# A gated hybrid block on one core: merge steps spread over half jobs, the last gate group as one job of four tiles, loads of y, x and A21 at other places

## The chip, the cores and the metric

The kernel runs on one core of a Trainium2 chip. The metric is device time in microseconds of one execution; the runs shown are three executions of the kernel before, and one more execution of it was profiled. Five engines work side by side on the core, each through its own instructions in order: TensorE (PE in the profile), VectorE (DVE), ScalarE (ACT), GpSimd (POOL) and SyncE (SP), which here only issues DMA transfers. One engine waits for another where an instruction needs what the other has not yet written, or a place that it has not yet freed.

## The reference

One layer over 512 tokens of width 2048, in float32. The normalised input is multiplied by a wide matrix `w_in`; its columns feed two mixers and their gates. Mixer A is a gated linear recurrence with 8 heads of 128. Mixer B is attention with 8 heads over keys that a small indexer picks, with a position bias. Both outputs are projected to 2048 columns, merged by sigmoid gates, projected once more, added to the input and normalised:

```
y_a = hgrn2_branch(a_q, a_f, a_i, a_g, lb_all[layer], gnorm_a[layer])
y_b = dsa_branch(c_q, c_kv, k_idx_raw, w_idx_raw, b_g, ..., w_ukv[layer], ..., rel_bias, topk)
merged = (jax.nn.sigmoid(m_a) * (y_a @ w_pa[layer])
          + jax.nn.sigmoid(m_b) * (y_b @ w_pb[layer]))
x = x + merged @ w_out[layer]
...
return rmsnorm(x, final_norm_w)
```

## The kernel before, in words

**Products.** Each float32 operand is split into a high part (a cast, ACT, L67) and a low part (a subtraction, DVE, L68), and each product is three matmuls: high by high, low by high, high by low (`mm3`, L71 to L73). Tiles of results hold 128 rows by 512 columns and lie in eight banks: four named acc and four others, from which the recurrence and the attention draw too.

**Weights.** All weights come in blocks of 512 KB, listed in `specs` in the order of use. `load` (L125) asks for a block on SP's queue; there are two places `wr` for raw blocks. `prep(i)`, called before block i is used, makes sure that the blocks up to i+2 are split (places `wh`, `wl`, three each) and that loads up to two blocks further are asked for. SP works through its queue in order: a transfer that must wait for its place holds up every transfer behind it.

**Jobs and lanes.** The program is a list of jobs, run one after the other. A job made by `feat_job` multiplies one group of weight columns (`ntile` tiles of 128) with the transposed input: for every block, for every tile, for every 128 rows k of the block, the three matmuls, and after every tile of a block one `pump()`. A pump advances each of six lanes by one step; a lane holds generators, and every `yield` is the end of a step. So the small work of the recurrence (`hgrn_gen`) and of the attention (`att_gen`) is put between the matmuls of the large jobs, one step per pump, and the matmuls between two pumps are the only work that PE has while the other engines carry out a step. In a job of two tiles with blocks of four k, there are 2 pumps per block and 12 matmuls between two pumps. Stores are asked for two pumps after the step that makes the data.

**The stages that the change touches.** The last input columns, four gate tiles (44 to 47), are made by two jobs of two tiles, each with four blocks of four k; during them the recurrence of the last pair of heads ends and the attention of pair 2 runs. Then `uqkv(3)` makes queries, keys and values of the last head pair (its second weight block is the only one from `w_ukv`). In the second gate job, after its second block, `end_x` (all steps of the recurrence are forced out) frees the places of the first half of the transposed input, and asks for all of `ya` (8 transfers of 512 KB) on SP's queue. Eight jobs of two tiles multiply with `w_pa`, and during the first of them the attention of the last pair runs. Eight jobs multiply with `w_pb`.

**Attention steps.** `att_gen` handles two heads of a pair, c = 0 and 1: `att_scores` (matmuls, maximum on DVE, two yields, Exp on ACT at L827, scale on DVE at L830), then two yields, then `att_turn` (transposes on PE, into banks tA, tB, tC, L841), two yields, `att_values`.

**Merge.** Each `w_pb` job has two tiles and two blocks, so four pumps, and 48 matmuls. Its evacuation `pb_evac` multiplies each tile with its gate (DVE, L1169, into `mg`), adds the tile of branch A on GpSimd (L1170), and puts `merge_pair` in the lane misc: three casts of the merged pair into operand tiles (ACT, L1143 to L1146), their low parts (DVE, L1145 to L1149), one step later four sums for the seven product scheme of the output (DVE, L1154 to L1157, `sv`), their cast and low part (`so`). `mg` has six places; each job uses four, loaded at L1106 by `load_gates`, which is listed after each job.

**Output.** `out_job` multiplies the merged matrix with `w_out`. The first 1536 columns are three column blocks, each of eight units of 42 matmuls of 256 columns: a scheme of seven products whose result tiles fill seven banks. `block_evac` combines them into `os`. The last 512 columns use eight more weight blocks; the last four are kept, so that the four token tiles end one after the other, and each is normalised and stored while the next is multiplied. For that, the remaining input columns `x` are loaded (`xr`) and added by `rest(t)`: one DVE addition of 1536 columns (L1255) and one ACT sum of squares (L1257). The low half operand A21 was written to memory by `merge_pair`, and is loaded back (L1234).

## Time and profile before

| quantity | value |
|---|---|
| three runs | 1454.05, 1455.7, 1457.64 us; median 1455.7 us |
| the profiled execution's own time | 1456.32 us |
| its span | 1454.5 us |
| mean granted clock of TensorE | 0.989 |
| PE busy | 1404.2 us (97% of the span) |
| DVE, ACT, POOL busy | 1055.6, 607.1, 114.1 us |
| HBM read, written | 163.63 MB, 31.99 MB |

By stage, from the view that sums each engine's busy time in stretches of the span:

| stretch of the span, us | what runs | PE busy | DVE busy | ACT busy | POOL busy |
|---|---|---|---|---|---|
| 986 to 1067 | two gate jobs, last uqkv | 75.32 | 45.89 | 35.75 | 14.01 |
| 1067 to 1168 | eight w_pa jobs | 98.67 | 47.30 | 29.59 | 7.20 |
| 1168 to 1261 | eight w_pb jobs | 90.97 | 56.35 | 30.30 | 17.77 |
| 1261 to 1277 | first units of out_job | 7.54 | 12.66 | 5.80 | 2.51 |
| 1277 to 1392 | the other units | 113.21 | 95.81 | 44.22 | 0.00 |
| 1392 to 1447 | last 512 columns, final norm | 48.49 | 30.02 | 21.02 | 0.00 |
| 1447 to 1454.5 | last stores | 0.00 | 1.93 | 2.54 | 0.00 |

In the rows of the timeline, the first number is when an instruction starts, in microseconds from the span's start, the second how long it takes (of a row with x2, the whole group), and the brackets hold how long the engine had been idle and what ended that. A busy PE may still run at a lower clock; the granted clock, 1.00 at full speed, stands in the view of stretches.

### The profile page before, as it was taken

To read this page: it belongs to the slowest core of one execution; us is meant where nothing else is said; L and a number is where in the kernel's file an instruction comes from. 1 tells how busy PE (TensorE), PEld (TensorE's weight loads), DVE (VectorE), ACT (ScalarE), POOL (GpSimd) and SP (SyncE) were. 2 spreads that over 40 slices of the span, in tenths; PEclk is the share of its full clock that TensorE was granted. 3 is DMA by queue.
4 is the path that set the end of the run, shared out by engine and by line. 5 is a ranking of instruction groups with operands and counts; after the bars stand their busy time and mean duration, and the time that the engine had idled before them with its cause. 6 is when DMAs were issued, how large, how long until landed. Compare 5 with 4: busy or idle time off the path is not lost.

```text
span 1454.5 us, 25789 instructions
## 1 busy us (share of the span) xinstructions
PE 1404.2 (97%) x10604; PEld 1278.5 (88%) x10604; DVE 1055.6 (73%) x1716; ACT 607.1 (42%) x856; POOL 114.1 (8%) x103
## 2 busy tenths in 40 slices
PE   7999999999999999999999999999989999799996
PEld 7888999999999999988989889888768887599985
DVE  6697888889888886776979757658445346789845
ACT  5545444444444443662252542544443123343334
POOL 3100000000000000000202203204010012100000
PEclk9999999999999999999999999999999999999998
DMA  6233344444444444335242342342575655533373
GB/s 209 74 90 112 113 120 145 131 130 145 132 132 131 132 121 126 101 99 154 65 125 81 109 130 85 112 127 78 188 276 173 202 176 187 173 105 113 115 276 130
DMA packets 140647, 197.30 MB, mean 136 GB/s; under 512 B 9793, under 2 KB 86130, under 8 KB 140402
## 3 DMA queue, kind: packets, MB, share of 16 engines
q1 hardware_dynamic: 139138, 193.48, 42.9%
q8 instruction: 83, 1.36, 0.4%
q10 hardware_dynamic: 1392, 2.18, 0.4%
q14 instruction: 34, 0.28, 0.1%
HBM read 163.63 MB, written 31.99 MB: 134 GB/s over the span
## 4 chain that ended last, share of the span: by engine, by line
PE 68%; DVE 16%; ACT 6%; DMA 5%; issue 3%; POOL 1%; SPq 1%; ACTq 0%; DVEq 0%; POOLq 0%
PE pp L71 10%; PE pp L73 10%; PE pp L72 10%; PE acc L71 9%; PE acc L72 9%; PE acc L73 9%; DVE wl L68 4%; ACT wh L67 2%; PE hl L76 1%; PE acc L76 1%; DMA mg<-gate_d 1%; POOL mg L1170 1%; DVE sv L138 1%; PE ho L76 1%; DMA wr<-in_w_ukv_dram 1%
## 5 line engine op out<-in xcount | busy, mean ns | idle before, releaser
L68 DVE TENSOR_TENSOR wl<-wr,wh 128x1024 fp32r<-128x1024 f32 x118 | 145.9, 1237 | 100.9 <-ACT wh L67 100.7
L67 ACT ACTIVATE wh<-wr 128x1024 fp32r<-128x1024 f32 x118 | 124.3, 1054 | 190.7 <-PE acc L73 54.3
L67 ACT ACTIVATE wh<-sv 128x1024 fp32r<-128x1024 f32 x112 | 118.4, 1057 | 165.1 <-DVE sv L140 152.6
L71 PE MATMUL acc<-xh,wh 128*128 128x512 f32 x432 | 173.2, 401 | 0.0
L73 PE MATMUL acc<-xh,wl 128*128 128x512 f32 x432 | 168.6, 390 | 0.0
L72 PE MATMUL acc<-xl,wh 128*128 128x512 f32 x432 | 168.2, 389 | 0.0
L68 DVE TENSOR_TENSOR wl<-sv,wh 128x1024 fp32r<-128x1024 f32 x112 | 137.3, 1226 | 27.4 <-ACT wh L67 27.2
L71 PE MATMUL pp<-sh,wh 128*128 128x256 f32 x528 | 149.7, 284 | 2.4 <-ACT c L483 1.7
L73 PE MATMUL pp<-sh,wl 128*128 128x256 f32 x528 | 149.5, 283 | 0.0
L72 PE MATMUL pp<-sl,wh 128*128 128x256 f32 x528 | 149.4, 283 | 0.0
L67 ACT ACTIVATE bh<-wr 128x768 fp32r<-128x768 f32 x112 | 94.0, 839 | 129.0 <-issue 59.2
L68 DVE TENSOR_TENSOR bl<-wr,bh 128x768 fp32r<-128x768 f32 x112 | 106.9, 954 | 31.3 <-ACT bh L67 30.5
L71 PEld LDWEIGHTS pp<-sh,wh 128*128 128x128 f32 x528 | 101.3, 192 | 3.1 <-ACT c L483 1.9
L73 PEld LDWEIGHTS pp<-sh,wl 128*128 128x128 f32 x528 | 101.3, 192 | 0.1
L72 PEld LDWEIGHTS pp<-sl,wh 128*128 128x128 f32 x528 | 101.3, 192 | 0.0
L73 PE MATMUL pp<-xh,bl 128*128 128x256 f32 x352 | 99.7, 283 | 0.5 <-DVE bl L68 0.5
L72 PE MATMUL pp<-xl,bh 128*128 128x256 f32 x352 | 99.6, 283 | 0.0
L71 PE MATMUL pp<-xh,bh 128*128 128x256 f32 x352 | 99.6, 283 | 0.0
L71 PEld LDWEIGHTS acc<-xh,wh 128*128 128x128 f32 x432 | 81.1, 188 | 18.0 <-issue 1.8
L73 PEld LDWEIGHTS acc<-xh,wl 128*128 128x128 f32 x432 | 81.1, 188 | 17.5
L72 PEld LDWEIGHTS acc<-xl,wh 128*128 128x128 f32 x432 | 81.2, 188 | 17.3 <-issue 1.4
L138 DVE TENSOR_TENSOR sv<-wr 128x512 f32<-128x512 f32 x112 | 76.9, 686 | 0.8
(385 smaller groups left out, 3729.0 us busy)
## 6 DMA issues: line engine op xcount, KB each, us to landing
wr<-in_w_in_dram SPq DMA_DIRECT2D x154, 512.0 KB, 3.7
wr<-in_w_out_dram SPq DMA_DIRECT2D x32, 512.0 KB, 3.8
mg<-gate_d SPq DMA_DIRECT2D x48, 256.0 KB, 3.4
gate_d<-c SPq DMA_DIRECT2D x44, 256.0 KB, 4.0
wr<-in_w_pa_dram SPq DMA_DIRECT2D x16, 512.0 KB, 5.6
wr<-in_w_pb_dram SPq DMA_DIRECT2D x16, 512.0 KB, 5.2
x<-in_x_dram SPq DMA_DIRECT2D x8, 512.0 KB, 6.8
wr<-in_w_qidx_dram SPq DMA_DIRECT2D x8, 512.0 KB, 4.2
```

Source lines behind the costliest of these rows:

```text
L67: A.activation(hi, src, AF.Copy)
L68: V.tensor_tensor(lo, src, hi.bitcast(F32), op=OP.subtract)
L71: PE.matmul(ps, lh, rh, start=first, stop=False, skip_group_check=True)
L72: PE.matmul(ps, lh, rl, start=False, stop=False, skip_group_check=True)
L73: PE.matmul(ps, ll, rh, start=False, stop=last, skip_group_check=True)
L76: PE.matmul(ps, l, r, start=first, stop=last, skip_group_check=True)
L138: V.tensor_tensor(sv[:, 0:2, :], b[:, 1:3, :], b[:, 0:1, :].to_broadcast([128, 2, 256]), op=OP.add)
L1170: G.tensor_tensor(u, u, g, op=OP.add)
```

## The change

1. `att_gen` has one more `yield` ahead of each `att_turn`.
2. The four gate tiles 44 to 47 are one job of four tiles with eight blocks of two k. There are four pumps per block, 32 in all, with 6 matmuls between two of them (before, 16 pumps with 12). The places of the transposed input come free after blocks 1, 3, 5 and 7, and `ya` is asked for in three parts: heads 0 to 3 after block 1, 4 and 5 after block 3, 6 and 7 after block 5, where the recurrence is forced out (`end_hgrn`).
3. `merge_pair` begins with a yield. The four sums come first (into a tile of `R.v0` instead of `sv`), then the casts; the cast of the sums and the low parts follow one step later, the sums' low part in the last step. The addition of branch A in `pb_evac` moves from GpSimd to DVE.
4. In `out_job`, the last 512 columns of `x` are asked for at its start. A21 is asked for after the third unit of the third column block, `x` for tile 0 and the norm's weights (now on SP's queue) after its fifth, `x` of tiles 1 and 2 after that column block, of tile 3 after `rest(0)`. `rest(0)` and `rest(1)` stand at the third and fourth weight block, `rest(2)` and `rest(3)` at the token tiles 0 and 1.

```diff
@@ att_gen
         MB = att_bias(2 * p + 1)
         yield
         yield
+        yield
         PT = att_turn(P)
...
         P = yield from att_scores(p, 1, MB)
+        yield
         yield
         yield
         PT = att_turn(P)
@@ gate_job
-    def gate_job(j0, after=None):
+    def gate_job(j0, after):
...
-        feat_job(w_in, GATE_COL[j0], 2, NK, 4, x_rhs, evac, after=after)
+        feat_job(w_in, GATE_COL[j0], 4, NK, 2, x_rhs, evac, after=after)
...
-    gate_job(44)
-    gate_job(46, {1: lambda: end_x(), 3: lambda: take_x("yb", 2)})
...
+    def end_hgrn():
         drain("hgrn")
         flush()
         flush()
         leave("hgrn")
         R.u = enter("us", side="right")
-        take_x("ya", 0)
-        load_y(R.ya, ya_d, 0, H)
+        load_y(R.ya, ya_d, 6, 8)
+
+    gate_job(44, {1: lambda: (take_x(R.ya, 0), load_y(R.ya, ya_d, 0, 4)),
+                  3: lambda: (take_x(R.ya, 1), load_y(R.ya, ya_d, 4, 6)),
+                  5: lambda: (end_hgrn(), take_x(R.yb, 2)),
+                  7: lambda: take_x(R.yb, 3)})
@@ merge_pair
+        d = R.v0.tile([128, 4, 256], F32, name="hv")
+        yield
+        V.tensor_tensor(d[:, 0, :], a21, a22, op=OP.subtract)
+        V.tensor_tensor(d[:, 2, :], a11, a21, op=OP.subtract)
+        V.tensor_tensor(d[:, 1, :], d[:, 0, :], a11, op=OP.subtract)
+        V.tensor_tensor(d[:, 3, :], d[:, 1, :], a12, op=OP.add)
         A.activation(mh[:, 0, :], a11, AF.Copy)
         A.activation(mh[:, 1:3, :], two, AF.Copy)
+        A.activation(last[0], a21, AF.Copy)
+        yield
+        A.activation(sums[:, 0], d, AF.Copy)
         V.tensor_tensor(ml[:, 0, :], a11, mh[:, 0, :].bitcast(F32), op=OP.subtract)
-        A.activation(last[0], a21, AF.Copy)
-        yield
         V.tensor_tensor(ml[:, 1:3, :], two, mh[:, 1:3, :].bitcast(F32), op=OP.subtract)
...
         yield
-        d = R.g.tile([128, 4, 256], F32, name="sv", bufs=R.sv)
...
-        split(sums[:, 0], sums[:, 1], d)
+        V.tensor_tensor(sums[:, 1], d, sums[:, 0].bitcast(F32), op=OP.subtract)
@@ pb_evac
             V.tensor_tensor(g, ps, g, op=OP.mult)
-            G.tensor_tensor(u, u, g, op=OP.add)
+            V.tensor_tensor(u, u, g, op=OP.add)
@@ out_job
+            def load_a21():
...
+            def load_ends():
+                load_rest(0, xpool, name="xr0", tag="xl1")
+                fw.append(xpool.tile([128, D], F32, name="fw", tag="xl0"))
+                SP.dma_start(fw[0], final_norm_w[None, :].to_broadcast([128, D]))
+
+            for t in range(4):
+                SP.dma_start(os[t][:, 1536:], x2[t * 128:(t + 1) * 128, 1536:])
             for cb in range(3):
-                pair_unit(at + cb * 8, NK // 2, lambda k: ms[k], block_evac(cb * 512), tokens_out=True)
+                pair_unit(at + cb * 8, NK // 2, lambda k: ms[k], block_evac(cb * 512), tokens_out=True,
+                          ahead={2: load_a21, 4: load_ends} if cb == 2 else {})
...
-            A.dma_start(fw, final_norm_w[None, :].to_broadcast([128, D]))
+            for t in (1, 2):
+                load_rest(t, R.o, name="xr", bufs=2)
...
-                if t < 2:
-                    load_rest(t + 2)
-
-            load_rest(0)
-            load_rest(1)
+                if t == 0:
+                    load_rest(3, xpool, name="xr3", tag="xl1")
+
...
-                rest(i)
+                if i >= 2:
+                    rest(i - 2)
             for t in range(4):
                 for i, w in enumerate(kept):
                     for k in (8 + 2 * i, 9 + 2 * i):
                         use(ps, w, k, t)
+                if t < 2:
+                    rest(t + 2)
```

What the diff does to the instructions is seen at three places. The first is ACT's queue around the end of the recurrence of the last pair (`hk` is its normaliser, `hy` the cast of its result) and the Exps of head c = 1 of pair 2 (`P`), whose transposes give `PT`. Before:

```order
L729 ACTIVATE hk<-hz,eps 128x512 x2
L730 ACT_TABLE_LOAD
L730 ACTIVATE hk<-hk 128x1024
L827 ACTIVATE P,sm<-P,mx 128x512
L827 ACTIVATE P,sm<-P,mx 128x384
L827 ACTIVATE P,sm<-P,mx 128x128
L827 ACTIVATE P,sm<-P,mx 128x256
L67 ACTIVATE wh<-wr 128x1024
L67 ACTIVATE hy_11367<-hk 128x512
L67 ACTIVATE hy_11371<-hk 128x512
L67 ACTIVATE PT<-tA 128x512
```

With the change:

```order
L729 ACTIVATE hk<-hz,eps 128x512 x2
L730 ACT_TABLE_LOAD
L730 ACTIVATE hk<-hk 128x1024
L67 ACTIVATE hy_11274<-hk 128x512
L67 ACTIVATE hy_11278<-hk 128x512
L827 ACTIVATE P,sm<-P,mx 128x512
L827 ACTIVATE P,sm<-P,mx 128x384
L827 ACTIVATE P,sm<-P,mx 128x128
L827 ACTIVATE P,sm<-P,mx 128x256
L67 ACTIVATE wh<-wr 128x1024
L67 ACTIVATE PT<-tA 128x512
```

The two casts of `hy`, which wait for DVE, now stand ahead of the four Exps instead of behind them, and a weight cast lies on the other side of the casts.

The second place is DVE's queue through one `w_pb` job, from the multiplication of one job's tiles by the gates to that of the next. Before:

```order
L1169 TENSOR_TENSOR mg<-acc,mg 128x512 x2
L1145 TENSOR_TENSOR ml_12620<-mg,mh_12619 128x256
L68 TENSOR_TENSOR wl<-wr,wh 128x1024
L1148 TENSOR_TENSOR ml_12620<-mg,mh_12619 128x512
L1149 TENSOR_TENSOR m21l<-mg,m21h 128x256
L1154 TENSOR_TENSOR sv<-mg 128x256
L1155 TENSOR_TENSOR sv<-mg 128x256
L1156 TENSOR_TENSOR sv<-sv,mg 128x256
L1157 TENSOR_TENSOR sv<-sv,mg 128x256
L68 TENSOR_TENSOR so_12623<-sv,so_12623 128x1024
L68 TENSOR_TENSOR wl<-wr,wh 128x1024
```

With the change, from the low part of the sums of one pair, ahead of which the first tile of the next job is already multiplied (L1180) and added (L1181):

```order
L1169 TENSOR_TENSOR so_12435<-hv,so_12435 128x1024
L1180 TENSOR_TENSOR mg<-acc,mg 128x512
L1181 TENSOR_TENSOR mg<-mg 128x512
L68 TENSOR_TENSOR wl<-wr,wh 128x1024
L1154 TENSOR_TENSOR hv<-mg 128x256
L1155 TENSOR_TENSOR hv<-mg 128x256
L1156 TENSOR_TENSOR hv<-hv,mg 128x256
L1157 TENSOR_TENSOR hv<-hv,mg 128x256
L1163 TENSOR_TENSOR ml_12526<-mg,mh_12525 128x256
L1164 TENSOR_TENSOR ml_12526<-mg,mh_12525 128x512
L1165 TENSOR_TENSOR m21l<-mg,m21h 128x256
L68 TENSOR_TENSOR wl<-wr,wh 128x1024
```

DVE has two additions more (L1181); the low part of the sums (`so`) of one pair stands between the two evacuations of the next job, and nothing in the row waits for GpSimd.

The third place is SP's queue around the weight block for the last keys and values (`w_ukv`). Before, the two loads of `ya` in the first rows are the last of four such pairs, which stand right behind each other:

```order
L1080 DMA yah<-ya_d 128x2x512
L1080 DMA yal<-ya_d 128x2x512
L125 DMA wr<-in_w_ukv_dram 128x2x512
L125 DMA wr<-in_w_pa_dram 128x4x256
L863 DMA yb_d<-ay_11472 128x512
L863 DMA yb_d<-ay_11473 128x512
```

With the change:

```order
L740 DMA ya_d<-hy_11279 128x512
L1082 DMA yh<-ya_d 128x2x512
L1082 DMA yl<-ya_d 128x2x512
L125 DMA wr<-in_w_in_dram 128x2x512
L863 DMA yb_d<-ay_11366 128x512
L863 DMA yb_d<-ay_11367 128x512
L125 DMA wr<-in_w_uq_dram 128x4x256
L1082 DMA yh<-ya_d 128x2x512
L1082 DMA yl<-ya_d 128x2x512
L125 DMA wr<-in_w_ukv_dram 128x2x512
```

Before, the `w_ukv` block stands behind eight loads of `ya` in a row; now behind two, and two other weight blocks and two stores stand ahead of those.

More of the change, by code (lines that the diff above doesn't have):

```diff
@@ L942, in pair_specs, with pair_unit @@
             specs.append(([(0, 512, src[k * 256:(k + 1) * 256, col:col + 512])], 2, 512, "pair"))
-    def pair_unit(at, n, rhs, evac, tokens_out=False):
+    def pair_unit(at, n, rhs, evac, tokens_out=False, ahead={}):
         pools7 = [(mmp, "acc"), (sdp, "sd")] * 3 + [(mmp, "acc")]
@@ L960, in pair_unit @@
             pump()
+            if k in ahead:
+                ahead[k]()
     def pair_job(src, col, n, rhs, evac):
@@ L1079, in load_y, with take_x @@
             for i in range(2):
-                SP.dma_start(y[i][h // 4][:, h % 4:h % 4 + 2, :].bitcast(F32), src[i, h:h + 2].rearrange("h p t -> p h t"))
-    def take_x(name, g0):
-        setattr(R, name, [[xpool.tile([128, 4, T], FR, name=f"{name}{a[1]}", tag=f"{a}{g0 + g}")
-                           for g in range(2)] for a in ("xh", "xl")])
-    def end_x():
+                SP.dma_start(y[i][h // 4][:, h % 4:h % 4 + 2, :].bitcast(F32),
+                             src[i, h:h + 2].rearrange("h p t -> p h t"))
+    R.ya, R.yb = ([[], []] for _ in range(2))
+    def take_x(y, g):
+        for i, a in enumerate(("xh", "xl")):
+            y[i].append(xpool.tile([128, 4, T], FR, name=f"y{a[1]}", tag=f"{a}{g}"))
+    def end_hgrn():
         drain("hgrn")
@@ L1142, in merge_pair @@
         two = u1.rearrange("p (a t) -> p a t", a=2)
+        d = R.v0.tile([128, 4, 256], F32, name="hv")
[4 more added lines that the diff above has]
+        V.tensor_tensor(d[:, 3, :], d[:, 1, :], a12, op=OP.add)
         A.activation(mh[:, 0, :], a11, AF.Copy)
         A.activation(mh[:, 1:3, :], two, AF.Copy)
-        V.tensor_tensor(ml[:, 0, :], a11, mh[:, 0, :].bitcast(F32), op=OP.subtract)
         A.activation(last[0], a21, AF.Copy)
         yield
+        A.activation(sums[:, 0], d, AF.Copy)
+        V.tensor_tensor(ml[:, 0, :], a11, mh[:, 0, :].bitcast(F32), op=OP.subtract)
         V.tensor_tensor(ml[:, 1:3, :], two, mh[:, 1:3, :].bitcast(F32), op=OP.subtract)
@@ L1219, in block_evac, with load_rest @@
                 return evac
+            a21, xr, fw = [], [], []
+            def load_a21():
+                for i in range(2):
+                    a21.append(xpool.tile([128, 8, 256], FR, name=f"a21{i}", tag=f"xh{i}"))
+                for k in (0, 4):
+                    for i in range(2):
+                        SP.dma_start(a21[i][:, k:k + 4, :].bitcast(F32), m21_d[i, :, k:k + 4, :])
+            def load_rest(t, pool, **kw):
+                xr.append(pool.tile([128, D], F32, **kw)[:, 0:1536])
+                SP.dma_start(xr[t], x2[t * 128:(t + 1) * 128, 0:1536])
+            def load_ends():
[4 more added lines that the diff above has]
+                SP.dma_start(os[t][:, 1536:], x2[t * 128:(t + 1) * 128, 1536:])
             for cb in range(3):
-                pair_unit(at + cb * 8, NK // 2, lambda k: ms[k], block_evac(cb * 512), tokens_out=True)
+                pair_unit(at + cb * 8, NK // 2, lambda k: ms[k], block_evac(cb * 512), tokens_out=True,
+                          ahead={2: load_a21, 4: load_ends} if cb == 2 else {})
             flush()
@@ L1226, in run @@
             leave("pairs")
+            fw = fw[0]
             R.o = enter("out", side="right")
-            fw = R.o.tile([128, D], F32, name="fw")
             ss = R.o.tile([128, 4, 3], F32, name="ss")
             r = R.o.tile([128, 4], F32, name="rfin")
-            a21 = [xpool.tile([128, 8, 256], FR, name=f"a21{i}", tag=f"xh{i}") for i in range(2)]
-            for k in (0, 4):
-                for i in range(2):
-                    SP.dma_start(a21[i][:, k:k + 4, :].bitcast(F32), m21_d[i, :, k:k + 4, :])
-            for t in range(4):
-                SP.dma_start(os[t][:, 1536:], x2[t * 128:(t + 1) * 128, 1536:])
-            A.dma_start(fw, final_norm_w[None, :].to_broadcast([128, D]))
+            for t in (1, 2):
+                load_rest(t, R.o, name="xr", bufs=2)
             def use(ps, w, k, t):
@@ L1245, in use @@
                 mm3(ps[t], *m, w[0][:, k % 2, :], w[1][:, k % 2, :], k == 0, k == NK - 1)
-            xr = []
-            def load_rest(t):
-                xr.append(R.o.tile([128, 1536], F32, name="xr", bufs=2))
-                SP.dma_start(xr[t], x2[t * 128:(t + 1) * 128, 0:1536])
             def rest(t):
```

4 lines of the change are left out of this document (removed).

## The prediction

> **What bounds the kernel now.** I read the page's busy times first, then the waits of PE, then stretches of the span around the long waits, and last the timeline at those places. The page says that PE sets the time nearly everywhere:
>
> ```profile
> PE 1404.2 (97%) x10604; PEld 1278.5 (88%) x10604; DVE 1055.6 (73%) x1716; ACT 607.1 (42%) x856; POOL 114.1 (8%) x103
> ```
>
> The change adds and removes no matmul. So it can win only what PE loses by waiting, and by the slower clock behind a wait. The view of PE's waits (what waited, on what: us in total, times, longest) names these losses at the places of the change:
>
> ```profile
> PE pp L71 <- DVE mg L1169: 7.8, 1, 7.8
> PE tA L841 <- DVE P L830: 5.8, 4, 1.9
> PE acc L71 <- ACT wk L67: 5.0, 2, 2.8
> PE acc L71 <- ACT gs L999: 3.5, 1, 3.5
> PE acc L72 <- DVE wk L68: 1.2, 2, 0.8
> PE acc L71 <- DVE ak L68: 0.6, 1, 0.6
> PE hl L76 <- POOL hk L666: 0.3, 1, 0.3
> ```
>
> A wait can cost twice. These stretches stand right behind three of them (stretch, length, busy times, then the granted clock ahead of the last two numbers):
>
> ```profile
> 1425.00:1430.00 5.00, 4.85 (x11) 3.80 (x12) 2.90 (x3) 0.00 (x0) 0.00 (x0) 0.50 0.01 3
> 1062.00:1065.00 3.00, 2.92 (x7) 2.37 (x8) 1.51 (x2) 2.44 (x5) 0.00 (x0) 0.50 0.62 182
> 1272.70:1276.70 4.00, 4.00 (x19) 4.00 (x20) 2.54 (x5) 1.78 (x4) 2.51 (x2) 0.50 0.18 70
> ```
>
> At a clock of 0.50 half of a stretch is lost: 1.5 us of the 3.0 behind the wait for `gs`, 2.0 of the 4.0 behind the one for `mg`. For the length of a matmul I take the first and the last of eleven in a row:
>
> ```profile
> 1027.80 0.39 PE L72 MATMUL acc<-xl,wh 128*128 128x512 f32 x1
> 1030.07 0.40 PE L73 MATMUL acc<-xh,wl 128*128 128x512 f32 x1
> ```
>
> Ten steps in 2.27 us are 0.227 us each. A pump of 12 matmuls covers 2.72 us, one of 6 covers 1.36 us.
>
> **The added pump ahead of the transposes.** The four waits for `P` sum to 5.8 us. One, in the gate jobs, is 1.93 us (quoted below) and belongs to the next part. The other three, 3.9 us, lie in jobs that keep 12 matmuls per pump; one more pump is 2.72 us of cover, and the longest of the three is below 1.93. So all three go: **3.9 us gained** (at least 2.8, if weight casts come to stand ahead of one of the Exps).
>
> **The gate job of four tiles.** Two things stand against each other here. The old losses first:
>
> ```profile
> 1059.06 1.06 ACT L67 ACTIVATE wh<-wr 128x1024 fp32r<-128x1024 f32 x1 [10.17 <-DMA wr<-in_w_ukv_dram]
> 1062.08 0.80 PE L71 MATMUL acc<-ckh,wh 128*128 128x512 f32 x1 [3.47 <-ACT gs L999]
> ```
>
> PE waited for `gs`, but ACT had stood 10.17 us for the `w_ukv` block, which lay behind 4 MB of `ya` on SP's queue; the cast and then the evacuation were queued behind it. With two loads ahead of the block in place of eight, asked for with a quarter of the job and the queries' matmuls still to go, that wait goes. With it go 1.5 us of half clock, and I count 0.6 (`ak`), 0.3 (`hk`) and 1.93 (`tA`) as replaced: 3.5 + 1.5 + 0.6 + 0.3 + 1.9 = 7.8 us removed.
>
> The new losses come from the pumps: the same steps of recurrence and attention now have 1.36 us of matmuls between them. The worst is at the transposes of c = 1:
>
> ```profile
> 1030.30 0.39 PE L76 MATMUL hz<-hzh,ones_r 128*128 128x512 f32 x1
> 1033.54 1.06 ACT L730 ACTIVATE hk<-hk 128x1024 f32<-128x1024 f32 x1
> 1034.51 0.71 ACT L827 ACTIVATE P<-P,mx 128x512 f32<-128x512 f32 x1
> 1036.60 0.19 ACT L827 ACTIVATION_READ_ACCUMULATOR P<-P,mx 128x1 f32 x1
> 1036.81 0.69 DVE L734 TENSOR_TENSOR hk<-hk,hg 128x512 f32<-128x512 f32 x1
> 1037.62 1.28 DVE L830 TENSOR_SCALAR P<-P,sm 128x512 f32<-128x512 f32 x4
> 1037.64 1.13 ACT L67 ACTIVATE hy<-hk 128x512 fp32r<-128x512 f32 x2
> 1038.78 0.72 PE L841 MATMUL tA<-ident,P 128*128 128x128 f32 x4 [1.93 <-DVE P L830]
> ```
>
> Before, the Exps ran right behind L730, beside DVE's work on `hk`. Now the two casts of `hy` stand ahead of them and wait for that work. The chain: 7.20 us from `hz` to the end of L734, 0.57 for the second cast, 2.28 for the Exps, about 1.6 for the reciprocal and L830: 11.65 us. PE has 4 `hz` and 24 other matmuls for that, 28 x 0.227 = 6.35. The wait is **5.3 us**, in place of 1.93. The second is on GpSimd:
>
> ```profile
> 988.65 3.62 POOL L796 TENSOR_TENSOR MB<-M,bh 128x256 f32<-128x256 f32 x3
> 992.23 1.10 POOL L666 TENSOR_TENSOR hk<-hk,tot 128x512 f32<-128x512 f32 x1
> ```
>
> One level of the recurrence has its product queued behind the bias additions, and is ready at 993.3. With half the matmuls on two pumps, PE gets there about 2.8 us earlier and waits 2.8. Four other steps (levels whose product takes 1.1 us or more plus the way there and back, against 1.36, and the states `hst`) I estimate at 0.4 to 0.7 each, 2.2 in all. For the clock behind the 5.3 us I put 1.75, the mean of the 1.5 and 2.0 above. New losses: 5.3 + 2.8 + 2.2 + 1.75 = 12.0, so **4.2 us lost** net. Bounds: 8 lost, if each of the five small waits is twice as long or the clock falls twice; 4 gained, if the casts of `hy` find DVE done sooner.
>
> [...]
>
> The DMA side I cost at nothing: the `ya` loads come between weight blocks that are asked for two blocks, 10.9 us, ahead of their cast. Without that cover, a cast would wait as long as the `xr` transfer below, 7.2 us.
>
> **Merge steps.** The `w_pb` stage and its end:
>
> ```profile
> 1169.31 0.39 PE L71 MATMUL acc<-ybh,wh 128*128 128x512 f32 x1
> 1260.72 0.34 PE L71 MATMUL pp<-bh,mh 128*128 128x256 f32 x1
> ...
> 1205.79 1.28 DVE L1169 TENSOR_TENSOR mg<-acc,mg 128x512 f32<-128x512 f32 x2
> 1206.61 2.53 POOL L1170 TENSOR_TENSOR mg<-mg 128x512 f32<-128x512 f32 x2 [9.80 <-DVE mg L1169]
> 1209.58 3.15 SPq L125 DMA_DIRECT2D wr<-in_w_pb_dram  x2
> 1215.73 1.04 ACT L67 ACTIVATE wh<-wr 128x1024 fp32r<-128x1024 f32 x1
> 1217.00 1.22 DVE L68 TENSOR_TENSOR wl<-wr,wh 128x1024 fp32r<-128x1024 f32 x1
> 1218.13 1.28 DVE L1169 TENSOR_TENSOR mg<-acc,mg 128x512 f32<-128x512 f32 x2
> ...
> wr<-in_w_pb_dram SPq DMA_DIRECT2D x16, 512.0 KB, 5.2
> ```
>
> Eight jobs are 384 matmuls, 87.1 us; they took 91.4, so 4.3 were lost inside. The evacuations come every 12.34 us, while PE needs 48 x 0.227 = 10.9: a loop through GpSimd, the casts, the sums and their cast makes each job later, PE runs ahead by its free banks and pays at the end, 7.85 us, and 2.0 of clock. Together 14.1 us.
>
> The change takes GpSimd's 2.53 out and puts two additions on DVE, 0.69 each by the row of L734. DVE's own work then fits in a job (about 9 of 10.9 us). What remains is a loop through SP's queue: the last L1181 frees a place, the load into it is asked for, the next `w_pb` block lies behind it. Its length: 0.44 (from the end of GpSimd's addition to SP's next block, before), 5.2 to land, 1.04 cast, 1.22 low part, then L1180, L1181, `so`, L1180, L1181, which are 0.64 + 0.69 + 1.22 + 0.64 + 0.69 = 3.9: 11.8 us, less some 0.1 at each of the DVE instructions that overlap: 11.3. That is 0.4 over PE; seven jobs give a lag of 2.8 us, which falls due at the first pair unit. So **11.3 us gained**, between 6 (a lag of 0.9 a job, with the clock) and 14.1 (none).
>
> **Output stage.** The stretch from the first of the last 512 columns' matmuls to the end of token tile 0, and DVE's rows in it:
>
> ```profile
> 1392.24 0.39 PE L71 MATMUL acc<-wh,mh 128*128 128x512 f32 x1
> 1430.01 0.55 PE L71 MATMUL acc<-wk,mh 128*128 128x512 f32 x1
> ...
> 1402.88 1.76 DVE L1255 TENSOR_TENSOR o<-o,xr 128x1536 f32<-128x1536 f32 x1 [7.22 <-DMA xr<-in_x_dram]
> 1439.43 1.75 DVE L1279 TENSOR_TENSOR o<-o,fw 128x1536 f32<-128x1536 f32 x1
> 1444.50 1.75 DVE L1279 TENSOR_TENSOR o<-o,fw 128x1536 f32<-128x1536 f32 x1
> 1446.70 0.42 DVE L1282 TENSOR_TENSOR o<-acc,o 128x256 f32<-128x256 f32 x1 [0.45 <-PE acc L73]
> ```
>
> Its 120 matmuls need 27.2 us and took 37.8: DVE stood at the first `rest` for `xr`, with the low parts of the weights queued behind it. 10.6 us are lost, clock included. Now `xr` is asked for some three units earlier (a unit is at most 131.5/24 = 5.5 us), and the first `rest` stands two blocks later, so the weights go first and PE should not wait. What comes back: `rest(3)` in tile 1. DVE needs 5.07 us per tile (1439.43 to 1444.50), PE 24 x 0.227 = 5.45; with 1.76 more DVE is 1.4 late there and recovers 0.4 per tile. I take 1.1 at the end (2.7 if `rest(2)` is in the way too): **9.5 us gained**, between 6 and 10.6. The earlier loads of `x` stand ahead of `w_out` blocks; two split blocks, about 10 us, cover them, and if not, the price is near the 7.2 us of the `xr` wait.
>
> **The sum.** Against the profiled execution's own 1456.3 us (its span of 1454.5 and 1.8 around it): 1456.3 - 3.9 + 4.2 - 11.3 - 9.5 = 1435.8. The median of the runs is 0.6 lower, so I forecast **1435 us**, by itself between 1428 and 1443.
>
> **Rivals.**
>
> *The load loop decides.* If the `w_pb` block and what is behind it still give 12.3 us per job, the lag is 7 x 1.4 = 10, plus 2 of clock, and 2 us of 14.1 are gained: **1444 us**. For it: SP works in order, and `w_pb` has among the longest landings. Against it: two blocks are always ahead, and the loop before had GpSimd in it.
>
> *Loads come no earlier.* SP's queue may keep `xr` and the weights behind the blocks of the third column block, and the 7.2 us wait stays: the tail gains about 2, **1443 us**. Against it: eight `w_out` blocks stand behind the first `xr` now, five before.
>
> *The dense pumps cost nothing.* If ACT and GpSimd find their inputs sooner than I think, 7.8 are gained in the gate job and the other terms come near their upper bounds: 1455.7 - 3.9 - 7.8 - 14.1 - 9.5 = **1420 us**. For it: ACT is busy 42% of the span and GpSimd 8%.
>
> *Slower: half clock through the gate job.* If the waits of 2.8 and 5.3 us, with the small ones between them, keep the clock at 0.50, the matmuls from the first to the end of the job, some 150 x 0.227 = 34 us, take 34 more; the waits, then covered, give 12 back. 1435 + 34 - 12 = 1457; it becomes slower than before once the half clock reaches over 33 us, and with the queries, keys and values of the last pair behind it, **1461 us**. For it: 0.50 for 5 us at 1425 with PE at work nearly all the time. Against it: at 1065 and 1277 the clock came back after 3 and 4 us.
>
> **How the numbers follow.** The forecast gets 0.57, the load loop 0.17, the late loads 0.08, the free pumps 0.13, half clock 0.05. The range 1424 to 1447 holds the forecast's whole band, most of the first two rivals, and the near side of the third. A measurement here can tell about 0.3%, 4.4 us. Slower: the half clock, 0.04. No change: its rest, and load loop and late loads together (about 1452), 0.05. Faster: 0.91.
>
> **What would show it.** Right: no wait of PE for `gs`, and none for `P` but one, of about 5 us, behind `hz`; evacuations of `w_pb` every 10.9 to 11.4 us and a wait below 4 us at the first pair unit; no wait for `wk`, and tile 0 ending some 27 us behind the last pair unit. Wrong: a `w_pb` period above 12, a granted clock of 0.5 over more than 6 us in the gate job, or DVE still waiting for `xr`.

## The result, and the profile after

The changed kernel takes 1430.53 us (median of six runs, 1430.2 to 1432.78) against 1455.39 us before (six runs): a ratio of 0.9832, interval 0.982 to 0.9845. That is 24.9 us less. The forecast was 1435 us with a range of 1424 to 1447: right in direction and size, 4.5 us too slow. The profiled execution has a span of 1430.7 us. One of the seven runs of the kernel before that stand beside the last four experiments took 4836 us; their ratios leave it out.

PE's busy time hardly moves; its waits are other ones. First the page's line of busy times, then the view of PE's waits after the change (what waited, on what: us in total, times, longest):

```profile
PE 1395.9 (98%) x10604; PEld 1276.9 (89%) x10604; DVE 1061.2 (74%) x1732; ACT 607.5 (42%) x855; POOL 91.8 (6%) x87
```

```profile
PE tA L841 <- DVE P L830: 4.8, 1, 4.8
...
PE hl L76 <- POOL hk L666: 2.5, 1, 2.5
...
PE pp L71 <- DVE mg L1180: 0.8, 1, 0.8
```

The rows for `gs`, for `wk` and for `ak` are gone, that for `mg` has shrunk from 7.8 to 0.8 us, and of four waits for `P` one is left, longer than any before. The 4.8 us and the 2.5 us for `hk` stand in the gate job.

Where the time went is seen best if the program is cut at PE's own milestones: the first matmul of each kind in the timeline. Each number is the time from one milestone to the next.

| from, to | before, us | after, us | difference |
|---|---|---|---|
| start, first keys and values (pair 0) | 803.26 | 804.25 | +1.0 |
| to those of pair 2 | 175.75 | 173.05 | -2.7 |
| to the first `w_pa` matmul (gate job, last `uqkv`) | 90.90 | 93.81 | +2.9 |
| to the first pair unit (`w_pa`, `w_pb`) | 190.81 | 184.17 | -6.6 |
| to the first matmul of the last 512 columns (24 units) | 131.52 | 121.47 | -10.1 |
| to the last matmul | 54.04 | 43.33 | -10.7 |
| to the end of the span | 8.22 | 10.62 | +2.4 |
| sum | 1454.5 | 1430.7 | -23.8 |

The first row is not of the change: in the twelve experiments it lies between 802.2 and 803.1 us. Of the 6.6 us in the fourth row, 2.3 lie in the `w_pa` jobs (1.6 of them are pair 3's wait for `P`) and 4.4 in the `w_pb` jobs.

**The gate job** became slower, as forecast. The timeline of the changed kernel shows how:

```profile
1018.30 0.39 PE L76 MATMUL hz<-hzh,ones_r 128*128 128x512 f32 x1
...
1021.71 1.06 ACT L730 ACTIVATE hk<-hk 128x1024 f32<-128x1024 f32 x1
1024.37 0.63 ACT L67 ACTIVATE hy<-hk 128x512 fp32r<-128x512 f32 x1 [1.60 <-DVE hk L734]
1025.70 0.63 ACT L67 ACTIVATE hy<-hk 128x512 fp32r<-128x512 f32 x1 [0.70 <-DVE hk L734]
1026.24 0.71 ACT L827 ACTIVATE P<-P,mx 128x512 f32<-128x512 f32 x1
...
1029.91 1.09 PE L841 MATMUL tA<-ident,P 128*128 128x128 f32 x4 [4.84 <-DVE P L830]
```

The two casts of `hy` wait for DVE in the brackets, and the Exps start only behind them. From `hz` to the transposes it is 11.6 us, and PE had matmuls for 6.8 of them. The view of stretches (the granted clock is the third number from the right) shows what followed, and, in its last row, that the other wait, the 2.5 us for `hk` which ended at 991.63, left the clock alone:

```profile
1030.00:1032.00 2.00, 2.00 (x11) 1.98 (x11) 1.16 (x2) 0.60 (x1) 0.00 (x0) 0.50 0.03 8
1032.00:1034.00 2.00, 2.00 (x7) 1.61 (x6) 1.62 (x3) 0.87 (x2) 0.00 (x0) 0.50 0.00 0
1034.00:1036.00 2.00, 2.00 (x8) 1.56 (x8) 0.00 (x0) 0.00 (x0) 0.00 (x0) 0.75 0.00 0
992.00:994.00 2.00, 2.00 (x54) 1.83 (x42) 1.57 (x2) 0.00 (x0) 1.47 (x1) 1.00 0.88 292
```

Four microseconds at 0.50 and two at 0.75 are 2.5 us lost. With 4.84, 2.45 and two small ones of 0.4 and 0.3, the new losses are 10.5 us against 7.8 removed: 2.7, nearly the +2.9 of the table. The clock stayed at 1.00 behind the 2.5 us here; in five of the experiments it stood at 0.50 behind the same wait, as the last section shows.

**The merge** no longer falls behind. The timeline of the changed kernel through one `w_pb` job:

```profile
1200.90 0.68 DVE L1180 TENSOR_TENSOR mg<-acc,mg 128x512 f32<-128x512 f32 x1
1204.08 0.69 DVE L1181 TENSOR_TENSOR mg<-mg 128x512 f32<-128x512 f32 x1
1205.22 1.10 SPq L125 DMA_DIRECT2D wr<-in_w_pb_dram  x2
1209.13 1.06 ACT L67 ACTIVATE wh<-wr 128x1024 fp32r<-128x1024 f32 x1 [0.66 <-DMA wr<-in_w_pb_dram]
1210.22 1.23 DVE L68 TENSOR_TENSOR wl<-wr,wh 128x1024 fp32r<-128x1024 f32 x1 [1.57 <-ACT wh L67]
1211.37 0.68 DVE L1180 TENSOR_TENSOR mg<-acc,mg 128x512 f32<-128x512 f32 x1
```

From one evacuation to the next it is 10.47 us here, and 10.57 on average over five jobs (1190.24 to 1243.06), below PE's 10.9; before it was 12.34. The loop is the one that the forecast named, with the next weight block behind the freed place, but the block is cast 3.9 us after it was asked for (3.8 to 4.2 in these five jobs); the forecast had 5.2 for its landing.

**The tail** has no wait of PE left, and a later end behind PE:

```profile
1386.49 1.06 ACT L67 ACTIVATE wh<-wr 128x1024 fp32r<-128x1024 f32 x1 [8.48 <-DMA wr<-in_w_out_dram]
...
1402.14 1.75 DVE L1276 TENSOR_TENSOR o<-o,xr 128x1536 f32<-128x1536 f32 x1
1403.81 1.75 DVE L1301 TENSOR_TENSOR o<-o,fw 128x1536 f32<-128x1536 f32 x1
1405.48 0.75 DVE L1304 TENSOR_TENSOR o<-acc,o 128x256 f32<-128x256 f32 x2
...
1422.89 0.75 DVE L1304 TENSOR_TENSOR o<-acc,o 128x256 f32<-128x256 f32 x2
```

PE's last matmul starts at 1420.08; DVE adds its tile only at 1422.89. Before, DVE waited for PE there (0.45 us at 1446.70). DVE is now the bound of the last tiles: `rest(2)` runs at 1402.14, when tile 0 is nearly done, and not during it. ACT's 8.48 us wait for a `w_out` block at the top made everything behind it late.

### The profile page after: what moved, and what is told of

The parts are those of the page before. It is cut to its first block, busy times and chain, and to the rows that moved or that the text cites. A ratio compares the mean times of both kernels' runs of the same rounds, so it can differ in the third digit from the quotient of the medians.

```text
span 1430.7 us, 25772 instructions
## 1 busy us (share of the span) xinstructions
PE 1395.9 (98%) x10604; PEld 1276.9 (89%) x10604; DVE 1061.2 (74%) x1732; ACT 607.5 (42%) x855; POOL 91.8 (6%) x87
## 4 chain that ended last, share of the span: by engine, by line
PE 69%; DVE 18%; ACT 6%; DMA 3%; issue 3%; POOL 0%; SPq 0%; ACTq 0%; DVEq 0%; POOLq 0%
PE acc L71 10%; PE pp L71 10%; PE acc L73 10%; PE acc L72 10%; PE pp L73 10%; PE pp L72 10%; DVE wl L68 3%; ACT wh L67 3%; DMA wr<-in_w_pb_dram 2%; DVE sv L138 1%; PE hl L76 1%; PE acc L76 1%; PE ho L76 1%; DVE sv L140 1%; DVE sv L139 1%
## 5 line engine op out<-in xcount | busy, mean ns | idle before, releaser
L71 PE MATMUL acc<-yh,wh 128*128 128x512 f32 x256 | 99.9, 390 | 0.0
L73 PE MATMUL acc<-yh,wl 128*128 128x512 f32 x256 | 99.7, 389 | 0.0
L72 PE MATMUL acc<-yl,wh 128*128 128x512 f32 x256 | 99.6, 389 | 0.0
```

Of the source, the lines that this page charges most:

```text
L71: PE.matmul(ps, lh, rh, start=first, stop=False, skip_group_check=True)
L72: PE.matmul(ps, lh, rl, start=False, stop=False, skip_group_check=True)
L73: PE.matmul(ps, ll, rh, start=False, stop=last, skip_group_check=True)
```

## The experiments

Each experiment ran beside runs of the kernel before on the same chip. Comparisons go by the ratio to these; the interval of each is 0.0015 to 0.002 to either side, 2 to 3 us, and where less than that is at stake the stages of the profile are read instead. The changed kernel is at 0.9832. In stages that an experiment doesn't touch, the first row apart, profiles differ from the changed kernel's by up to 1.4 us, once by 2.4; where the difference is above 1 us in the gate stage, and in the case of 2.4, the clock stood at 0.50 for 3.4 us more.

### The pumps: two runs on the gate job, one on the attention

**Attention steps as before.** Both added yields are taken out of the changed kernel (the lines show one of the two places):

```diff
-        yield
         yield
         yield
         PT = att_turn(P)
```

> The changed kernel with the two added pumps ahead of the transposes taken out again; the rest stays. Theory (each pump covers a chain that is otherwise short by 1.1 to 1.9 us): waits of PE for P come back at heads of pairs 0, 1 and 3, 1.1 + 1.2 + 1.6 = 3.9 us, and the 4.84 us wait in the gate job grows by one pump of 1.36 us: 1430.5 + 3.9 + 1.4 = 1436 us. Rival (the waits only move to the next step that PE needs): within 1.5 us of the changed kernel.

Ratio 0.9868 (0.9854 to 0.9883), 1437.29 us against 1456.59 before: 0.36% or 5.2 us above the changed kernel, as the theory has it. The sum is right, the places are not quite. The view of PE's waits:

```profile
PE tA L841 <- DVE P L830: 7.2, 4, 4.5
```

In order of time these are 1.2, 1.2, 0.2 and 4.5: pairs 0 and 1 return, the gate job's waits spread over more steps, and pair 3's 1.6 us does not return. That wait goes with the places of the loads: ACT's cast of a `w_pa` block, behind which these Exps stand, starts 10.9 us after the first `w_pa` matmul here, and 14.2 us after it before the change.

**Two short jobs, loads in three parts.** This separates the shape of the gate job from the places of its loads:

```diff
-        feat_job(w_in, GATE_COL[j0], 4, NK, 2, x_rhs, evac, after=after)
+        feat_job(w_in, GATE_COL[j0], 2, NK, 4, x_rhs, evac, after=after)
...
+    gate_job(44)
+    gate_job(46, {0: lambda: (take_x(R.ya, 0), load_y(R.ya, ya_d, 0, 4)),
+                  1: lambda: (take_x(R.ya, 1), load_y(R.ya, ya_d, 4, 6)),
+                  2: lambda: (end_hgrn(), take_x(R.yb, 2)),
+                  3: lambda: take_x(R.yb, 3)})
```

> The changed kernel with the four gate tiles as two jobs of two tiles and blocks of four k again, but ya still asked for in three parts (behind blocks 0, 1 and 2 of the second job) and all else as changed. Theory (the short pumps make the waits of 4.84 and 2.45 us, the small ones and about 2.5 us of half clock; the loads' places alone remove the wait for the w_ukv block): no wait for P or hk above 0.5 us, none for gs, 1430.5 - 10.5 = 1420 us. Rival (the job of four tiles is what takes the w_ukv wait away, since x comes free evenly in it): the wait for gs of about 3.5 us and 1.5 us of half clock come back, 1425 us. Third: the waits are fixed by the chains and only move, 1430 us.

Ratio 0.9779 (0.9763 to 0.9795), 1424.15 us: 7.7 us below the changed kernel. The gate stage takes 83.40 us instead of 93.81, just the 10.4 that the theory gives, with no wait for `gs` and the clock at 1.00 throughout, here from 1000 us on:

```profile
1000.00:1030.00 30.00, 30.00 (x171) 26.02 (x170) 16.19 (x35) 14.68 (x24) 4.31 (x5) 1.00 0.22 67
1030.00:1059.00 29.00, 28.76 (x146) 24.14 (x145) 16.83 (x26) 16.97 (x29) 0.00 (x0) 1.00 0.92 317
```

So the loads' places alone remove the `w_ukv` wait; in this stage the job of four tiles brought only losses. 2.6 us come back in the next stage, which the theory had not: `ya` and `yb` now lie closer together, `w_pa` blocks behind them, and PE waits for an attention product:

```profile
PE po L72 <- DVE P L68: 1.4, 1, 1.4
```

**The job of four tiles, two pumps more for pair 2.** The lines show one of the two places:

```diff
         yield
         yield
         yield
+        for _ in range(2 if p == 2 else 0):
+            yield
         PT = att_turn(P)
```

> The changed kernel, job of four tiles and all, with two pumps more ahead of each transpose of pair 2 (the pair that runs in the gate job). Theory (the 4.84 us wait is matmuls missing between hz and the transposes, and the half clock follows it): the wait goes, the clock stays at 1.00 behind it, the 2.45 us wait for hk stays: 1430.5 - 4.8 - 2.5 = 1423 us. Rival (the half clock comes from the small waits and low density of this job, not from the one wait): 1425.7 us, with the clock still at 0.5 somewhere in the job.

Ratio 0.981 (0.9794 to 0.9826), 1427.81 us: 3.2 us below the changed kernel by the timing, with runs from 1425.8 to 1430.6. The mechanism is clear in the profile, whose gate stage is 5.6 us shorter (88.22): the wait at the transposes is 1.2 us instead of 4.8, the 2.5 us for `hk` stay, and the clock is 1.00 in every stretch:

```profile
1020.00:1030.00 10.00, 10.00 (x46) 8.04 (x45) 7.76 (x22) 5.24 (x13) 0.00 (x0) 1.00 0.56 198
1030.00:1040.00 10.00, 8.77 (x48) 7.54 (x48) 5.79 (x12) 3.90 (x6) 0.00 (x0) 1.00 0.53 186
```

The half clock at the transposes follows the one long wait; without it, it is gone. Of the 7.3 us expected, 1.2 stay as a wait. By the timing alone the rival's 1425.7 us is nearer than the theory's 1423; it is the clock in the profile that speaks against the rival.

### The merge: each half of the edit alone

**Addition on GpSimd, new steps.**

```diff
-            V.tensor_tensor(u, u, g, op=OP.add)
+            G.tensor_tensor(u, u, g, op=OP.add)
```

> The changed kernel with the addition of branch A back on GpSimd; the new order of the merge stays. Theory of the prediction (GpSimd's 2.5 us are in the loop that sets the period of a w_pb job): period 11.3 to 11.9 us instead of 10.6, a lag of 0.4 to 1.0 us in each of seven jobs, paid at the first pair unit: 1433 to 1438 us. Rival (the new order of sums and casts alone took the loop below PE's 10.9 us, GpSimd's part is covered): within 1.5 us of 1430.5.

**Old steps, addition on DVE.** Here `merge_pair` is that of before: casts first, sums one step later, split at once.

```diff
-        d = R.v0.tile([128, 4, 256], F32, name="hv")
-        yield
-        V.tensor_tensor(d[:, 0, :], a21, a22, op=OP.subtract)
...
+        d = R.g.tile([128, 4, 256], F32, name="sv", bufs=R.sv)
+        V.tensor_tensor(d[:, 0, :], a21, a22, op=OP.subtract)
...
+        split(sums[:, 0], sums[:, 1], d)
```

> The changed kernel with the old steps of merge_pair (casts first, sums one step later, their split at once); the addition of branch A stays on VectorE. Theory that the order counts: the loop of before, 12.34 us, only loses what the addition is shorter (0.82 + 2.53 against 4 x 0.65): about 11.6 us per job, a lag of 0.7 x 7 = 5 us at the first pair unit and perhaps 2 us of clock, less the 0.8 us paid already: 1434 to 1437 us. Rival (GpSimd alone made the loop): within 1.5 us of 1430.5.

Ratios 0.9902 (0.9887 to 0.9917, 1442.15 us) and 0.9885 (0.9866 to 0.9904, 1440.47 us): each half alone is 8 to 10 us slower than both together. Neither rival holds; it is not one part that did it. Both theories were too low as well, at most 1438 and 1437 us. The periods, first with GpSimd and the new steps, then with DVE and the old:

```profile
1193.56 0.68 DVE L1180 TENSOR_TENSOR mg<-acc,mg 128x512 f32<-128x512 f32 x1
1205.34 0.69 DVE L1180 TENSOR_TENSOR mg<-acc,mg 128x512 f32<-128x512 f32 x1
...
1208.85 0.42 DVE L1154 TENSOR_TENSOR hv<-mg 128x256 f32<-128x256 f32 x1 [1.18 <-POOL mg L1181]
...
1267.91 0.58 PE L71 MATMUL pp<-wh,so 128*128 128x256 f32 x1 [5.69 <-DVE mg L1180]
```

```profile
1191.05 0.68 DVE L1178 TENSOR_TENSOR mg<-acc,mg 128x512 f32<-128x512 f32 x1
1202.78 0.68 DVE L1178 TENSOR_TENSOR mg<-acc,mg 128x512 f32<-128x512 f32 x1
...
1266.18 0.58 PE L71 MATMUL pp<-wh,so 128*128 128x256 f32 x1 [7.86 <-DVE mg L1178]
```

| merge | period of a job, us | wait at the first pair unit | from the first `w_pa` matmul to the last columns, us |
|---|---|---|---|
| old steps, GpSimd (before) | 12.3 to 12.4 | 7.85 | 322.3 |
| new steps, GpSimd | 11.8 to 13.3 | 5.69 | 314.8 |
| old steps, DVE | 11.7 | 7.86 | 314.5 |
| new steps, DVE (changed) | 10.6 | 0.78 | 305.6 |

PE needs 10.9 us per job. Each half takes some 0.6 us off the loop at best, and while the period is above 10.9 the lag grows with every job and is paid at the first pair unit, with a slower clock behind it (0.50 from 1266 to 1270 with GpSimd). Both together take the loop below PE's, and the lag does not form. (2.3 us of the step from 322.3 lie in the `w_pa` jobs, 1.6 of them the wait for `P` of pair 3, in all three.) The expectation for the old steps was 11.6 us per job, and 11.7 was measured, but its price was set too low: 5 us for the lag and perhaps 2 for the clock, where the stage shows 8.9.

### The tail: loads and places

**Rest one place earlier.**

```diff
-                if i >= 2:
-                    rest(i - 2)
+                if i >= 1:
+                    rest(i - 1)
...
-                if t < 2:
-                    rest(t + 2)
+                if t < 1:
+                    rest(t + 3)
```

> The changed kernel with every rest one place earlier: rest(0) to rest(2) behind weight blocks 1 to 3, rest(3) at token tile 0. Theory (DVE is late at the end, by 2.4 us behind PE's last matmul, because rest(2) and rest(3) lie in tiles 0 and 1, while DVE stood 7.4 us idle for weights before): one rest less in the tiles, end earlier by 1.4 to 1.8 us, 1429 us. Rival (the last four tiles' own work, about 5 us per tile, sets the end): no change. Second rival: rest(0) now holds up the weights' low parts behind it, PE waits again, 1433 us or more.

**Rest at its old places, loads at the new ones.**

```diff
-                if i >= 2:
-                    rest(i - 2)
+                rest(i)
...
-                if t < 2:
-                    rest(t + 2)
```

> The changed kernel with rest(0) to rest(3) at weight blocks 0 to 3 as before the change, with the loads at their new places. Theory (the late xr load was what stopped DVE; with the loads early the old places are as good or better): no wait of PE for weights' low parts, DVE free in the tiles, 1428 to 1430 us. Rival (the places of rest count for themselves: xr of tile 0 is there, but those of tiles 1 to 3 come behind w_out blocks, and DVE waits in front of the weights): PE waits 3 us or more in this stage, 1434 us or more.

**Loads at their old places, rest at the new ones.**

```diff
-                          ahead={2: load_a21, 4: load_ends} if cb == 2 else {})
+                          )
...
+            load_a21()
+            for t in range(4):
+                SP.dma_start(os[t][:, 1536:], x2[t * 128:(t + 1) * 128, 1536:])
+            A.dma_start(fw, final_norm_w[None, :].to_broadcast([128, D]))
...
+            load_old(0)
+            load_old(1)
```

> The changed kernel with the loads of A21, x and the norm's weights back at their old places (behind the last pair unit), and rest at its new places. Theory (both are needed: the first rest waits for xr until about 10 us behind the last pair unit, now one or two weight blocks sooner than DVE needs it): a smaller part of the 10.7 us returns, 2 to 5 us, 1433 to 1436 us. Rival (the places of rest are the whole gain, since at the third block xr is there in any case): within 1.5 us. Other rival (the loads are the whole gain): 1439 us or more.

Ratios 0.9848 (1434.52 us), 0.985 (1435.39 us) and 0.9885 (1440.0 us). All three missed their theories. Rests at earlier places are 2.3 and 2.6 us slower, near the edge of the interval, but the stage is clear: the rivals in which PE waits again hold. With the loads at their old places 7.7 us are lost, not 2 to 5; that is near the rival in which the loads are the whole gain. From the first matmul of the last columns to the end of the span:

| loads, places of rest | us |
|---|---|
| old, old (before) | 62.3 |
| old, new | 61.2 |
| new, old | 57.5 |
| new, one earlier | 58.1 |
| new, new (changed) | 54.0 |

The loads alone are worth 4.8 us, the places alone 1.1, both 8.3. Why an earlier rest hurts is in the timeline of the run with rest one place earlier:

```profile
1386.24 1.23 DVE L68 TENSOR_TENSOR wl<-wr,wh 128x1024 fp32r<-128x1024 f32 x1 [7.78 <-ACT wh L67]
1387.38 1.75 DVE L1276 TENSOR_TENSOR o<-o,xr 128x1536 f32<-128x1536 f32 x1
1389.17 1.49 ACT L1278 ACTIVATE junk<-o 128x1536 bf16<-128x1536 f32 x1 [2.96 <-DVE o L1276]
1390.66 1.04 ACT L67 ACTIVATE wk<-wr 128x1024 fp32r<-128x1024 f32 x1
1391.73 1.23 DVE L68 TENSOR_TENSOR wk<-wr,wk 128x1024 fp32r<-128x1024 f32 x1 [2.60 <-ACT wk L67]
...
1402.84 0.80 PE L71 MATMUL acc<-wk,mh 128*128 128x512 f32 x1 [2.86 <-ACT wk L67]
```

Addition (DVE), squares (ACT), the next weight's cast (ACT), its low part (DVE): one chain of 1.75 + 1.49 + 1.04 + 1.23 us, each waiting for the one before, 5.5 us per weight block with the ways between. PE uses up a block in 5.45 us. So a delay at the start of this chain is not made up, and here the chain starts one block too soon: PE waits 2.86 us, and the granted clock is 0.50 from 1403 to 1407. In the changed kernel two weights are split ahead of the first rest (at 1387.58 and 1388.83; the rest starts at 1389.97), so PE does not wait.

**Loads of tiles 1 and 2 behind the first weight preparation.** The delay at the start of the chain is the 8.48 us wait of ACT for a `w_out` block. The end follows it one for one: in the five experiments that leave the tail as changed, this wait is 7.24 to 8.80 us, and the end lies 2.0 to 2.3 us more than the wait behind PE's last matmul (9.35 to 10.80). Two `xr` loads, 1.5 MB, stand ahead of it; they are put behind:

```diff
                 prep(at + 24 + i)
+                if i == 0:
+                    for t in (1, 2):
+                        load_rest(t, R.o, name="xr", bufs=2)
```

> The changed kernel; the loads of x for token tiles 1 and 2 are asked for behind the first preparation of the last eight weight blocks instead of ahead of it. Theory (these 1.5 MB stand ahead of a w_out block on SP's queue, so that ACT waits 8.5 us for it, and every later weight and rest is late by that, which is why rests at earlier places made PE wait for a weight and why DVE ends 2.4 us behind PE): the wait for w_out shrinks to 4 to 5 us and the end comes 1 to 2 us sooner, about 1429 us on a chip where the changed kernel takes 1430.5. Rival (the end is bound by DVE's own work in tiles 0 and 1, whenever the weights come): no change.

**And the rest in two parts.** The additions move to blocks 1 to 3 and tile 0, the squares one step behind them:

```diff
-                if i >= 2:
-                    rest(i - 2)
+                if i >= 2:
+                    square(i - 2)
+                if i >= 1:
+                    rest(i - 1)
...
                 if t < 2:
-                    rest(t + 2)
+                    square(t + 2)
+                if t == 0:
+                    rest(3)
```

> As the run before it, and each rest is parted: the addition on DVE one weight block earlier (blocks 1 to 3 and token tile 0), the sum of squares on ACT one step behind it, so that the cast of the next weight on ACT does not wait for DVE's addition. Theory (cast, low part, addition, squares are one chain of 5.5 us per weight, as long as PE's 5.4, so no delay is ever made up; parted, it is about 3 us): no wait of PE for weights although the additions come earlier, and DVE's last addition follows PE by less than 1 us: 1428 us. Rival: PE waits for a weight again as with the earlier rests, 1433 us.

Ratios 0.9833 (0.9815 to 0.985) and 0.9822 (0.9807 to 0.9838): by the timing neither can be told from the changed kernel's 0.9832. The profiles tell them apart: from PE's last matmul to the end it is 9.4 us with the moved loads, and 8.2 us, the value of before, with the parted rest; PE takes the same 43.3 us in both. With the moved loads ACT waits 4.4 us there, for a place and no longer for a block, and the first rest starts 2.2 us sooner; but the end gains only 1.2, as the additions of `rest(2)` and `rest(3)` still stand in tiles 0 and 1. With the parted rest ACT no longer stands behind DVE's addition, and DVE waits for PE again at the end:

```profile
1381.88 1.75 DVE L1274 TENSOR_TENSOR o<-o,xr 128x1536 f32<-128x1536 f32 x1
1383.46 1.06 ACT L67 ACTIVATE wk<-wr 128x1024 fp32r<-128x1024 f32 x1 [2.75 <-DMA wr<-in_w_out_dram]
1384.55 1.23 DVE L68 TENSOR_TENSOR wk<-wr,wk 128x1024 fp32r<-128x1024 f32 x1 [0.91 <-ACT wk L67]
...
1417.73 0.76 DVE L1312 TENSOR_TENSOR o<-acc,o 128x256 f32<-128x256 f32 x2 [0.45 <-PE acc L73]
```

### A version better than both

**Two short gate jobs with ya in three parts, and the parted tail.**

> The gate tiles as two jobs of two tiles with ya in three parts, and the tail of the run before it. Theory: the gains add, 1430.5 - 7.5 (gate part, as measured) - 2.4 (tail) = 1420.5 us. Rival (tail gain is lost): 1423 us.

**The same, yb asked for behind the third w_pa job.**

```diff
-    jobs.append(lambda: load_y(R.yb, yb_d, 0, 6))
...
         feat_job(w_pa, j * 128, 2, H, 4, y_rhs("ya"), pa_evac(j))
+        if j == 4:
+            jobs.append(lambda: load_y(R.yb, yb_d, 0, 6))
```

> As the run before it, with the loads of yb (3 MB) asked for behind the third w_pa job instead of ahead of the first. Theory (with the two short jobs the w_pa stage lost 2.6 us, 1.4 of it a wait for an attention product whose cast on ACT stood behind a w_pa block, and that block behind yb on SP's queue): the wait goes, 2 us less than the run before. Rival (w_pa's blocks are late for the gates' and ya's traffic): no change.

The first is at 0.9771 (0.9755 to 0.9786), 1420.82 us; on the scale of the forecast that ratio is 1422.1, too near both the theory (1420.5) and the rival (1423) to choose. The stages do: the gate stage takes 83.6 us, and the last columns to the end 51.5, against 53.7 with the short jobs alone. So the gains add. The second is at 0.975 (0.9734 to 0.9765), 1418.0 us against 1454.61 before, 2.8 us less than the first on the same chip. Its stage from the first `w_pa` matmul to the first pair unit takes 184.2 us again, not 186.8; the wait for the attention product is gone, and in that stage PE is never idle (second row: the pair units):

```profile
1060.00:1244.00 184.00, 184.00 (x836) 153.27 (x836) 112.13 (x186) 61.65 (x88) 6.44 (x8) 1.00 0.66 214
1244.00:1365.00 121.00, 119.15 (x1010) 118.53 (x1009) 102.46 (x154) 46.47 (x54) 0.00 (x0) 1.00 0.46 150
```

## Why the prediction was right, and where it was off

**Attention pumps: 3.9 us forecast, about 4 measured, a third of it by another cause.** The runs without the added pumps give back 5.2 us with the gate job's share. Pairs 0 and 1 are as forecast: their waits return without the pumps. Pair 3's 1.6 us went through the places of the loads: I had put down as a matter of pumps a wait whose Exps stood behind a cast that waited for a `w_pa` block.

**Gate job: 4.2 us lost forecast, 2.9 lost.** Its steps hold one by one: no wait for `gs`, 5.3 us forecast at the transposes and 4.84 measured, 2.8 for `hk` and 2.45 measured, clock 1.75 and 2.5 measured. The four small waits were sized too high, 2.2 us where 0.7 came. What the clock did behind a wait did not follow from its length alone. In the changed kernel's own trace 2.45 us left it at 1.00 and 4.84 us were followed by 6.8 us at 0.50; but the same wait for `hk`, 2.46 to 2.50 us, was followed by 3.4 us at 0.50 in five of the nine other runs that have it. There the gate stage takes 94.1 to 95.2 us, up to 4.3 more than before. The forecast put a price on the clock behind the longer wait alone; by these runs a second one, behind the wait for `hk`, was as likely as not, and the 2.9 of this one profile is partly luck.

**Merge: 11.3 us forecast, 14.4 measured** (10.1 at the pair units and 4.4 in the `w_pb` jobs). The mechanism was right, the rival of the load loop wrong, and the mis-sized term is the landing of the `w_pb` block: 5.2 us, where it was cast 3.8 to 4.2 us after the request. The 5.2 is the landing of one block, asked for at 1149.86 among the `w_pa` jobs; for the other 15 the profile gives none. The rest of the loop was put a little low, 6.1 us for 6.5. Together that put the loop at 11.3 us instead of 10.6, on the wrong side of PE's 10.9, and a lag of 2.8 us into the sum where 0.8 came. The two half edits show how much hangs on that side: at 11.7 us and more the stage takes 9 us longer.

**Tail: 9.5 us forecast, 8.3 measured** (10.7 to the last matmul, 2.4 given back behind it). PE's part was right. The step that failed is "1.1 at the end": I let `rest(2)` run under tile 0, with the weights long split; the 2.7 that I put in brackets for the other case was the better price. They were not split: ACT had waited 8.48 us for a block behind the `xr` loads, and each rest then took its 5.5 us in turn. The two tail runs show both parts of it: 1.2 us come back with the moved loads, and 1.2 more with the parted and earlier rest.

**The slower rival** needed a half clock over 33 us; it lasted 6.8. The rival in which the short pumps cost nothing is excluded by the two short jobs: the job of four tiles costs 10.4 us, more than the 5.0 us (3.5 of wait and 1.5 of clock) that its loads gained.

**The forecast as a whole** was 4.5 us too slow: 3.1 by the merge, 1.3 by the gate job, 0.4 by the attention's waits and 0.6 in the `w_pa` jobs that no term had and that I did not trace, less 1.2 by the tail.

## What to carry to other kernels

A loop over several engines that runs beside PE cost 0.8 us here with its period at 10.6 us, below PE's 10.9, and grew a debt in every turn at 11.7 and more. So compare the two periods before valuing any part of the loop; half an edit may get less than half the gain. Where small dependent steps are spread between matmuls, halving the matmuls between steps halves the cover of every chain: change the places of loads and the grain of the steps separately, since here the loads held the gain and the grain only cost. And where a chain alternates between two in-order engines, a step with work on both is worth parting, so that the next weight's cast does not stand behind the last result's sum.
